# RWKV-7 scan of a two-layer diffusion backbone: r stored beside the keys, the values' chunk halves exchanged when they are written, the in-context rates of both directions in one tensor

## The chip, the cores and the metric

The kernel runs on one core of a Trainium2 chip. The metric is the device time of one launch, in microseconds (us); lower is better. The time before the change is 2466.11 us, the median of three runs (2457.85, 2466.11 and 2469.48). Engines are named as the profile names them: PE (TensorE matmuls) and PEld (its weight loads), DVE (VectorE), ACT (ScalarE), POOL (GpSimd) and SP (SyncE, which here issues nearly all transfers; its rows in the trace are marked SPq).

## What is computed

Layer 0 is attention, layer 1 is a bidirectional RWKV-7 time mixing beside a Hyena convolution. All arithmetic is float32. The change touches layer 1's RWKV branch alone: 8 heads of width 64, 1024 latent tokens behind 256 context tokens, both directions. Cut to what matters:

```python
def rwkv_features(u, w0, w_up, a0, a_up, k_k, k_a):
    r, k, v, dw_f, dw_b, da_f, da_b = split_cols(u, RWKV_SPLITS)
    kk = to_heads(k * k_k, RWKV_HEADS)
    kk = kk * lax.rsqrt(jnp.sum(kk * kk, axis=-1, keepdims=True) + 1e-12)
    for d, (dw, da) in enumerate(((dw_f, da_f), (dw_b, da_b))):
        w_log = -jax.nn.softplus(-(w0[d] + jnp.tanh(dw) @ w_up[d])) - 0.5
        decay = jnp.exp(-jnp.exp(w_log))
        a = jax.nn.sigmoid(a0[d] + da @ a_up[d])
        k_d = k * (1 + (a - 1) * k_a)
        dirs.append((decay, k_d, kk * a))
...
    def step(s, inp):                       # wkv_scan, per token, either direction
        sa = jnp.einsum('bhij,bhj->bhi', s, kk_t)
        s = s * w_t[:, :, None, :] - sa[..., None] * b_t[:, :, None, :] + v_t[..., None] * k_t[:, :, None, :]
        y = jnp.einsum('bhij,bhj->bhi', s, r_t) if emit else None
...
    yn = (yn * gn_w + gn_b)                 # rwkv_readout: group norm over a head, then the bonus
    bonus = jnp.sum(r * k_bonus * r_k, axis=-1, keepdims=True) * v
```

The context is scanned first; its final state starts the scan of the latent tokens. `k_bonus` is the mean of both directions' `k_d`, so the bonus needs r, k, v and both directions' a.

## The kernel before

The program is one instruction stream per engine, put in order ahead of the run by a scheduler that simulates a timeline and lists the ready instructions; a change in any transfer can therefore move instructions of all engines that follow it. Layer 1 ends with two stages that overlap.

**Projection (`gemm3`).** 128-column blocks of the input projection. `rw` makes one block of r, v or k after the token shift and writes it to DRAM. Blocks of v and r go to `US` (features by tokens, line 1125). Keys go through `rw_keys` to `KK`, a tensor [512 features, 5 blocks, 2, 256 tokens], where slot 0 holds the normalised keys kk and slot 1 the keys k (line 1318). `rw_values` transposes v to tokens by features and writes `VT` (line 1331). `rw_gates` writes the sigmoids of the decay (`SG`, one tensor per direction) and the in-context rates a (`AS`, one tensor per direction).

**Scan (`rwkv`).** There are 8 jobs, 4 head pairs j by 2 directions d, each of 5 blocks of 256 tokens (block 0 is the context): 40 blocks in all. Every block goes through

- `rw_front` (lines 1464 to 1576): loads kk and k (`kkf`, line 1475) and for the latent blocks r (line 1477), a (`af`), the decay (`sg`) and the values `V` (line 1486); makes chunk matrices of 64 tokens on PE, DVE, ACT and POOL; writes 32x32 blocks of the triangular system to DRAM (`LD`, line 1558). `V` is wanted with the two 64-token chunks of every 128 tokens exchanged between the halves of the partitions, and so is loaded by two transfers of 64 partitions;
- `rw_invert` (line 1578): reads the small blocks of a job back (`L<-LD`, line 1588) and inverts them by a loop of 31 steps on DVE, two instructions a step (`tmp`, line 1595, and `X`, line 1597); writes `XD` (line 1599). Job 0 is inverted in two parts, blocks 0 and 1 and then blocks 2 to 4;
- `rw_inverses` (line 1606): four loads of the inverse, `XT`; `rw_solve`: the solve (`y_ps`, `z_ps`, `R` on DVE at line 1629, `w_ps`), which also loads the values in both halves of `UV` (line 1617);
- `rw_trans`, `rw_own` and `rw_scan`: the transition matrices and the state's recurrence (`sy_ps` on PE, `S` on ACT), four chunks a block.

Up to 12 fronts run ahead of the scan. For the 16 latent blocks of direction 1, `rw_bonus` (line 1709) loads k, a of direction 0, a of direction 1, r, v and the gate g (line 1718), each as a tile of its own: `iok`, `ioa`, `iob` and `ior` share four buffers. POOL forms the bonus keys (lines 1721 to 1724), DVE multiplies r (line 1725), PE sums over a head (`bo_ps`). `rw_readout` normalises and, for j below 3, writes the high and the low half of the result by two transfers (line 1770). From block 28 on `Final` runs the output projection (`fe_ps`) between the scans.

SP issues its transfers in program order. A load whose buffer is still read holds everything behind it on SP.

Of the kernel before, what the change touches and what calls it, by code (L numbers as in the profile page):

```python
# [10 lines left out]
F32 = mybir.dt.float32  # L11
# [164 lines left out]
class K:  # L176
# [39 lines left out]
    def dt(self, shape, name, dt=F32):  # L216
        return self.dram.tile(shape, dt, name=name, tag=name)
# [781 lines left out]
    def layer1(self):  # L999
        nc, tc, a = self.nc, self.tc, self.a  # L1000
        dt = self.dt
        self.US = dt([13 * 128, NT], "US")
        self.G1 = dt([512, NL], "G1")
        self.HT = [dt([2, 8, 128, 512], "HT0"), dt([8, 128, 512], "HT1")]
        self.HF = dt([512, 4, 256], "HF")
        self.M1 = dt([2, 1024, NL], "M1")
        self.XC = dt([2, 128, KT, NC_], "XC")
        self.KK = dt([512, 5, 2, 256], "KK")
        self.VT = dt([NT, 512], "VT")
        self.AS = [dt([512, NT], f"AS{d}") for d in range(2)]  # L1010
        self.SG = [dt([NT, 512], f"SG{d}") for d in range(2)]
        with ExitStack():
            with ExitStack() as s2:
                xp = s2.enter_context(tc.tile_pool(name="l1x", bufs=1, reuse_waits="tile"))
                xl = [xp.tile([128, KT, NL], F32R, name=f"xl{p}") for p in range(2)]
                cst = ExitStack()
                xp = cst.enter_context(tc.tile_pool(name="l1c", bufs=1, reuse_waits="tile"))
                self.xc = [xp.tile([128, KT, NC_], F32R, name=f"xc{p}") for p in range(2)]

                def x(p, k, t0, n):  # L1020
                    return self.xc[p][:, k, t0:t0 + n] if t0 < NC_ else xl[p][:, k, t0 - NC_:t0 - NC_ + n]

                with ExitStack() as s3:
                    wp = s3.enter_context(tc.tile_pool(name="adap1", bufs=1, reuse_waits="tile"))
                    pp = s3.enter_context(tc.tile_pool(name="adaps1", bufs=2, space=PSUM, reuse_waits="tile"))
                    self.gemm2(x, wp, pp)
                self.wo_stack.close()
                for p in range(2):
                    nc.sync.dma_start(out=self.XC[p], in_=self.xc[p].bitcast(F32))
                cst.close()  # L1030
                self.gemm3(x)
            if self.stop == "gemm3":
                return
            self.rwkv()
# [21 lines left out]
    def gemm3(self, x):  # L1056
# [3 lines left out]
        with ExitStack() as st:  # L1060
# [44 lines left out]
            def rw(c0, b, ctx, w, sub):  # L1105
# [16 lines left out]
                if b // 4 == 1:  # L1122
                    self.rw_keys(b - 4, o, rp, pp)
                else:
                    nc.sync.dma_start(out=self.US[c0:c0 + 128, 0 if ctx else NC_:], in_=o)
                if b // 4 == 2:
                    self.rw_values(b - 8, o, rp, pp)

# [172 lines left out]
    def rw_keys(self, j, o, sp, pp):  # L1301
# [13 lines left out]
            nc.gpsimd.tensor_tensor(out=kk[:, s], in0=kk[:, s], in1=sq[:, 0:n], op=ALU.mult)  # L1315
        rows = slice(j * 128, j * 128 + 128)
        for i, t in enumerate((kk, o)):
            nc.sync.dma_start(out=self.KK[rows, :, i, :], in_=t.rearrange("p (q t) -> p q t", t=256))

    def rw_values(self, j, o, sp, pp):  # L1320

# [3 lines left out]
        for t4 in range(0, 10, 4):  # L1325
# [2 lines left out]
            for q in range(m):  # L1328
                nc.tensor.matmul(ps[:, q, :], o[:, (t4 + q) * 128:(t4 + q + 1) * 128], self.cent, start=True, stop=True)
            self.evac(vt[:, t4:t4 + m, :], ps[:, 0:m, :])  # L1330
        nc.sync.dma_start(out=self.VT[:, j * 128:j * 128 + 128].rearrange("(t p) f -> p t f", p=128), in_=vt)

    def rw_gates(self, sp, pp):

# [129 lines left out]
    def rw_front(self, F, q, wp, bufs):  # L1464
# [7 lines left out]
        K0 = math.exp(-0.5)  # L1472

        kk = fp.tile([128, 3, 256], F32, name="kkf", bufs=2)
        nc.sync.dma_start(out=kk[:, 1:3], in_=self.KK[rows, q])
        if lat:
            nc.sync.dma_start(out=kk[:, 0], in_=self.US[rows, q * 256:q * 256 + 256])
        af = fp.tile([128, 256], F32, name="af", bufs=3)
        nc.sync.dma_start(out=af, in_=self.AS[d][rows, q * 256:q * 256 + 256])
        sg = fp.tile([128, 2, 128], F32, name="sg", bufs=3)  # L1480
        tok = slice(q * 256, q * 256 + 256)
        nc.sync.dma_start(out=sg, in_=self.SG[d][tok, rows].rearrange("(t p) f -> p t f", p=128))
        V = fp.tile([128, 2, 128], F32, name="V", bufs=2)
        vsrc = self.VT[tok, rows].rearrange("(i c p) f -> c p i f", c=2, p=64)
        for c in range(2):
            nc.sync.dma_start(out=V[64 * c:64 * c + 64], in_=vsrc[1 - c])
        sgs = fp.tile([128, 2, 2, 128], F32R, name="sgs", bufs=2)
        self.split(sgs[:, 0], sgs[:, 1], sg)

# [118 lines left out]
    def rw_solve(self, F, q, n):  # L1608
# [5 lines left out]
        rows = slice(F["j"] * 128, F["j"] * 128 + 128)  # L1614
        vsrc = self.VT[q * 256:q * 256 + 256, rows].rearrange("(i c p) (h f) -> c p i h f", c=2, p=64, h=2)
        for c in range(2):
            nc.sync.dma_start(out=UV[64 * (1 - c):64 * (1 - c) + 64, :, c], in_=vsrc[c])

        def prod(w, x, name):
            ps = self.rps([128, 4, 128], name, "s", PB[0])  # L1620
# [88 lines left out]
    def rw_bonus(self, j, q):  # L1709
# [1 line left out]
        nc, C, wp = self.nc, self.C, self.wp  # L1711
        rows, tok = slice(j * 128, j * 128 + 128), slice(q * 256, q * 256 + 256)
        io = []
        for n, src in (("k", self.KK[rows, q, 1, :]), ("a", self.AS[0][rows, tok]), ("b", self.AS[1][rows, tok]),
                       ("r", self.US[rows, tok]), ("v", self.US[1024 + j * 128:1152 + j * 128, tok]),
                       ("g", self.G1[rows, q * 256 - 256:q * 256])):
            t = wp.tile([128, 256], F32, name=f"io{n}", tag="iovg" if n in "vg" else "io", bufs=4)
            nc.sync.dma_start(out=t, in_=src)
            io.append(t)
        k, a0, a1, r, v, g = io  # L1720
        nc.gpsimd.tensor_tensor(out=a0, in0=a0, in1=a1, op=ALU.add)
        nc.gpsimd.tensor_scalar(out=a0, in0=a0, scalar1=0.5, scalar2=-1.0, op0=ALU.mult, op1=ALU.add)
        nc.gpsimd.tensor_scalar(out=a0, in0=a0, scalar1=self.col("rwkv_k_a", j), scalar2=1.0, op0=ALU.mult, op1=ALU.add)
# [7 lines left out]
    def rw_readout(self, j, q, Y, vg):  # L1731
# [31 lines left out]
        if j == 3:  # L1763
            m = self.m3[q]
            self.split(m[:, 0], m[:, 1], t)
            return
        m = [wp.tile([128, 256], F32R, name="m1", tag="m1", bufs=3) for _ in range(2)]
        self.split(m[0], m[1], t)
        for p in range(2):
            nc.sync.dma_start(out=self.M1[p, j * 128:j * 128 + 128, q * 256 - 256:q * 256], in_=m[p].bitcast(F32))  # L1770


    def reduced_sin(self, out, ps, bias, pool):
# [398 lines left out]
```

## Time and profile before

| what | us |
|---|---|
| median of three runs | 2466.11 |
| the profiled execution's own time | 2463.09 |
| its span (first to last instruction) | 2461.3 |
| PE busy in the span | 2212.4 (90%) |
| PEld / DVE / ACT / POOL busy | 1839.0 / 1548.4 / 1103.4 / 927.3 |

The page's shares are averages over stages with different limits. The scan's fronts begin at about 1763 us, the first solve at about 1861 us, the output projection mixes in from about 2250 us. A view by stages (stretches of time with each engine's busy time, the granted PE clock as a part of full speed, and the DMA engines' mean busy share) tells them apart. The chain of waits follows the work that ended last back from the last instruction; a piece "SPq L1477" in it is the time in which SP issued that transfer, and "DMA kkf<-US" the time from the issue to its landing.

### The profile page before, as it was taken

The page shows a single profiled execution, that of the slowest core. Times are in us where ns is not written, and L with a number is a line of the kernel's source. Part 1 is how long each engine was busy: PE and PEld are TensorE (multiplying, and loading weights), DVE is VectorE, ACT ScalarE, POOL GpSimd, SP SyncE. Part 2 cuts the span into 40 slices and gives each one's busy share as a digit, 9 for nine tenths or more (in the row PEclk, how much of TensorE's full clock was granted, in tenths as well). Part 3 has the DMA queues.
Part 4 walks back from the last instruction along what each step waited for, and adds up shares of the span by engine and source line. Part 5 has one row for each costly group of instructions (what it writes and reads, how often), then busy time and mean ns, then how long its engine had stood idle before and what let it go on. Part 6 is the DMA issues. An engine that isn't in the chain of part 4 may idle for free. (4 is left out here: it accounts for less than half of the span.)

```text
span 2461.3 us, 45979 instructions
## 1 busy us (share of the span) xinstructions
PE 2212.4 (90%) x17167; PEld 1839.0 (75%) x17167; DVE 1548.4 (63%) x3091; ACT 1103.4 (45%) x2403; POOL 927.3 (38%) x959
## 2 busy tenths in 40 slices
PE   4999999999999998689899999899968888988897
PEld 3877788677877887577788787788756777777685
DVE  6255532368768877454476877566788886767524
ACT  5354434456556555532232232255444455555224
POOL 1253335301011545511132333323564555556512
PEclk8999999999999999899999999999968899998898
DMA  8433344673222666834443464474443444444522
GB/s 283 133 124 118 125 144 146 194 234 121 85 74 70 193 196 185 241 116 168 154 146 119 147 207 145 152 237 154 146 130 86 129 126 127 114 129 134 172 84 93
DMA packets 351573, 361.79 MB, mean 147 GB/s; under 512 B 83122, under 2 KB 283199, under 8 KB 350582
## 3 DMA queue, kind: packets, MB, share of 16 engines
q1 hardware_dynamic: 342038, 330.40, 44.3%
q10 hardware_dynamic: 9168, 24.25, 3.2%
q0 software_dynamic: 144, 4.19, 0.4%
q8 instruction: 136, 2.23, 0.4%
q14 instruction: 87, 0.71, 0.1%
HBM read 260.14 MB, written 100.10 MB: 146 GB/s over the span
## 5 line engine op out<-in xcount | busy, mean ns | idle before, releaser
L160 PE MATMUL g_ps<-xl,w_hi 128*128 128x512 f32 x1056 | 269.0, 401 | 1.0 <-ACT w_hi L194 1.0
L160 PEld LDWEIGHTS g_ps<-xl,w_hi 128*128 128x128 f32 x1056 | 200.1, 192 | 44.6 <-issue 2.4
L160 PE MATMUL s_ps<-k,q 128*128 128x256 f32 (+1 forms) x704 | 199.1, 379 | 7.3 <-DVE pn L702 4.0
L443 POOL TENSOR_TENSOR al_acc<-al_acc,al_t 128x512 f32<-128x512 f32 x98 | 128.8, 1314 | 186.5 <-ACT al_t L441 135.9
L198 DVE TENSOR_TENSOR w_lo<-w_raw,w_hi 128x256 fp32r<-128x256 f32 (+1 forms) x184 | 126.8, 745 | 85.3 <-PE g_ps L160 44.2
L189 ACT COPY pt<-pt_ps 128x512 f32<-128x512 f32 (+1 forms) x203 | 101.7, 505 | 137.6 <-PE pt_ps L163 131.7
L1595 DVE TENSOR_TENSOR tmp<-L,X 80x112 f32<-80x112 f32 (+28 forms) x279 | 136.9, 491 | 25.4 <-DMA L<-LD 17.0
L1597 DVE TENSOR_TENSOR X<-X,tmp 80x112 f32<-80x112 f32 (+28 forms) x279 | 136.1, 488 | 6.6
L160 PE MATMUL g_ps<-xl,w_lo 128*128 128x512 f32 x528 | 137.4, 394 | 0.0
L163 PE MATMUL pt_ps<-ident,p 128*128 128x128 f32 x704 | 119.2, 285 | 17.0 <-DVE pt L187 7.1
L160 PE MATMUL g_ps<-xhi,w_hi 128*128 128x512 f32 (+1 forms) x528 | 118.3, 366 | 8.9 <-DVE ac_res L285 4.7
L163 PEld LDWEIGHTS pt_ps<-ident,p 128*128 128x128 f32 x704 | 81.6, 143 | 52.5 <-DVE pt L187 14.2
L160 PEld LDWEIGHTS s_ps<-k,q 128*128 128x128 f32 x704 | 108.9, 198 | 14.5 <-DVE p L702 7.3
L697 ACT ACTIVATE p<-p,mn 128x1280 f32<-128x1280 f32 (+1 forms) x96 | 103.4, 1078 | 35.7 <-DVE p L702 35.6
L160 PE MATMUL g_ps<-xhi,w_lo 128*128 128x512 f32 (+1 forms) x528 | 119.0, 364 | 0.0
L883 POOL TENSOR_TENSOR bias<-namask,tt 128x384 f32<-128x384 f32 x64 | 67.7, 1059 | 129.9 <-DVE mn L892 54.1
L441 ACT ACTIVATE al_t<-al_w,condT 128x512 f32<-128x512 f32 x98 | 70.8, 722 | 98.9 <-POOL al_acc L443 62.3
L160 PEld LDWEIGHTS g_ps<-xl,w_lo 128*128 128x128 f32 x528 | 98.9, 189 | 20.9 <-issue 0.7
L160 PE MATMUL g_ps<-xlo,w_hi 128*128 128x512 f32 (+1 forms) x528 | 113.0, 356 | 0.0
L160 PEld LDWEIGHTS g_ps<-xhi,w_hi 128*128 128x128 f32 x528 | 89.9, 193 | 29.6 <-DVE qraw L551 5.4
L160 PEld LDWEIGHTS g_ps<-xhi,w_lo 128*128 128x128 f32 x528 | 89.8, 191 | 18.9 <-issue 5.8
L160 PEld LDWEIGHTS g_ps<-xlo,w_hi 128*128 128x128 f32 x528 | 89.6, 191 | 15.8 <-issue 1.9
(432 smaller groups left out, 5708.4 us busy)
## 6 DMA issues: line engine op xcount, KB each, us to landing
w_raw<-rec_w_in SPq DMA_DIRECT2D x33, 512.0 KB
hfw<-FW SPq DMA_DIRECT2D x32, 512.0 KB
w_raw<-attn_w_in SPq DMA_DIRECT2D x13, 1024.0 KB
al_w<-rec_ada_w SPq DMA_DIRECT2D x48, 256.0 KB
tt<-TG SPq DMA_DIRECT2D x64, 192.0 KB
kkf<-KK SPq DMA_DIRECT2D x40, 256.0 KB
q<-qb SPq DMA_DIRECT2D x64, 128.0 KB
HS<-hs SPq DMA_DIRECT2D x32, 256.0 KB
```

The lines of the kernel that those rows point to most:

```text
L160: return self.keep(self.pe.matmul(*args, **kw))
L163: return self.keep(self.pe.transpose(*args, **kw))
L189: self.nc.scalar.copy(out=out, in_=in_)
L198: e.tensor_tensor(out=lo, in0=full, in1=hi.bitcast(F32), op=ALU.subtract)
L441: nc.scalar.activation(out=o, in_=wt, func=AF.Copy, scale=self.condT[:, k, ci:ci + 1])
L443: nc.gpsimd.tensor_tensor(out=t, in0=t, in1=o, op=ALU.add)
L697: self.nc.scalar.activation(out=p, in_=p, func=AF.Exp, bias=mn, scale=-1.0, accum_out=rs)
L883: nc.gpsimd.tensor_tensor(out=b, in0=mask, in1=tt, op=ALU.subtract)
L1595: nc.vector.tensor_tensor(out=tv, in0=L[:, s:s + 1, rt].to_broadcast([n, nj, nt]), in1=X[:, rj, s:s + 1].to_broadcast([n, nj, nt]), op=ALU ...
L1597: nc.vector.tensor_tensor(out=X[:, rj, rt], in0=X[:, rj, rt], in1=tv, op=ALU.subtract)
```

## The change

1. `KK` becomes [512, 5, 3, 256]: slot 0 takes r (latent blocks only), slots 1 and 2 kk and k. The four r blocks are written there rather than to `US`. A latent front loads r, kk and k by one transfer of 384 KB, where it loaded 256 KB and 128 KB.
2. The chunk halves are exchanged when `VT` is written (two transfers of 64 partitions in place of one of 128, four times). A front loads `V` by one transfer of 128 partitions; `UV` still takes two, with the halves named the other way round.
3. `AS` becomes one tensor [2, 512, tokens]. The bonus loads r and k by one transfer and both rates by one: four transfers of 128 KB become two of 256 KB, into two buffers of twice the size.
4. The readout's high and low halves go out by one transfer (tile `m1`, two buffers of 256 KB for three of 128 KB).

```diff
-        self.KK = dt([512, 5, 2, 256], "KK")
+        self.KK = dt([512, 5, 3, 256], "KK")
-        self.AS = [dt([512, NT], f"AS{d}") for d in range(2)]
+        self.AS = dt([2, 512, NT], "AS")
...
-                    nc.sync.dma_start(out=self.US[c0:c0 + 128, 0 if ctx else NC_:], in_=o)
+                    if ctx:
+                        nc.sync.dma_start(out=self.US[c0:c0 + 128, :], in_=o)
+                    else:
+                        nc.sync.dma_start(out=self.KK[c0:c0 + 128, 1:5, 0, :], in_=o.rearrange("p (q t) -> p q t", t=256))
...
-            nc.sync.dma_start(out=self.KK[rows, :, i, :], in_=t.rearrange("p (q t) -> p q t", t=256))
+            nc.sync.dma_start(out=self.KK[rows, :, i + 1, :], in_=t.rearrange("p (q t) -> p q t", t=256))
...
-        nc.sync.dma_start(out=self.VT[:, j * 128:j * 128 + 128].rearrange("(t p) f -> p t f", p=128), in_=vt)
+        for c in range(2):
+            nc.sync.dma_start(out=self.VT[:, j * 128:j * 128 + 128].rearrange("(t c p) f -> c p t f", c=2, p=64)[1 - c],
+                              in_=vt[64 * c:64 * c + 64])
...
-        nc.sync.dma_start(out=kk[:, 1:3], in_=self.KK[rows, q])
-        if lat:
-            nc.sync.dma_start(out=kk[:, 0], in_=self.US[rows, q * 256:q * 256 + 256])
+        nc.sync.dma_start(out=kk if lat else kk[:, 1:3], in_=self.KK[rows, q] if lat else self.KK[rows, q, 1:3])
...
-        vsrc = self.VT[tok, rows].rearrange("(i c p) f -> c p i f", c=2, p=64)
-        for c in range(2):
-            nc.sync.dma_start(out=V[64 * c:64 * c + 64], in_=vsrc[1 - c])
+        nc.sync.dma_start(out=V, in_=self.VT[tok, rows].rearrange("(i p) f -> p i f", p=128))
...
-            nc.sync.dma_start(out=UV[64 * (1 - c):64 * (1 - c) + 64, :, c], in_=vsrc[c])
+            nc.sync.dma_start(out=UV[64 * (1 - c):64 * (1 - c) + 64, :, c], in_=vsrc[1 - c])
...
-        for n, src in (("k", self.KK[rows, q, 1, :]), ("a", self.AS[0][rows, tok]), ("b", self.AS[1][rows, tok]),
-                       ("r", self.US[rows, tok]), ("v", self.US[1024 + j * 128:1152 + j * 128, tok]),
-                       ("g", self.G1[rows, q * 256 - 256:q * 256])):
-            t = wp.tile([128, 256], F32, name=f"io{n}", tag="iovg" if n in "vg" else "io", bufs=4)
+        for n, src in (("rk", self.KK[rows, q, 0:3:2, :]), ("ab", self.AS[:, rows, tok].rearrange("d p t -> p d t"))):
+            t = wp.tile([128, 2, 256], F32, name=f"io{n}", tag="io", bufs=2)
+            nc.sync.dma_start(out=t, in_=src)
+            io += [t[:, 0], t[:, 1]]
+        for n, src in (("v", self.US[1024 + j * 128:1152 + j * 128, tok]), ("g", self.G1[rows, q * 256 - 256:q * 256])):
+            t = wp.tile([128, 256], F32, name=f"io{n}", tag="iovg", bufs=4)
             nc.sync.dma_start(out=t, in_=src)
...
-        m = [wp.tile([128, 256], F32R, name="m1", tag="m1", bufs=3) for _ in range(2)]
-        self.split(m[0], m[1], t)
-        for p in range(2):
-            nc.sync.dma_start(out=self.M1[p, j * 128:j * 128 + 128, q * 256 - 256:q * 256], in_=m[p].bitcast(F32))
+        m = wp.tile([128, 2, 256], F32R, name="m1", tag="m1", bufs=2)
+        self.split(m[:, 0], m[:, 1], t)
+        nc.sync.dma_start(out=self.M1[:, j * 128:j * 128 + 128, q * 256 - 256:q * 256].rearrange("p f t -> f p t"), in_=m.bitcast(F32))
```

What the change does to the order is shown at three places. Line numbers are each kernel's own: in the changed one `kkf` is loaded at line 1481, `af` at 1483, `sg` at 1486, `V` at 1488, `UV` at 1619, the bonus at 1718 and 1722, and the readout writes at 1773. A number behind a name (`AS_12036`) tells tensors of one name apart.

**SP, the loads of the first two fronts (a context block, then a latent one).** Before:

```order
L1475 DMA kkf<-KK 128x512
L1479 DMA af<-AS_12036 128x256
L1482 DMA sg<-SG_12038 128x2x128
L1486 DMA V<-VT 64x2x128 x2
L1475 DMA kkf<-KK 128x512
L1477 DMA kkf<-US 128x256
L1479 DMA af<-AS_12036 128x256
L1482 DMA sg<-SG_12038 128x2x128
L1486 DMA V<-VT 64x2x128 x2
```

Now:

```order
L1481 DMA kkf<-KK 128x512
L1483 DMA af<-AS 128x256
L1486 DMA sg<-SG_12037 128x2x128
L1488 DMA V<-VT 128x2x128
L1483 DMA af<-AS 128x256
L1481 DMA kkf<-KK 128x768
L1486 DMA sg<-SG_12037 128x2x128
L1488 DMA V<-VT 128x2x128
```

A latent front now has four loads on SP where it had six.

**SP, around the fourth bonus of job 1 (in the trace at about 1955 us), up to its load of the rates.** Before:

```order
L1475 DMA kkf<-KK 128x512
L1477 DMA kkf<-US 128x256
L1479 DMA af<-AS_12037 128x256
L1486 DMA V<-VT 64x2x128 x2
L1606 DMA XT_17594<-XD_17621 32x4x32 x4
L1475 DMA kkf<-KK 128x512
L1479 DMA af<-AS_12036 128x256
L1718 DMA ioa<-AS_12036 128x256
L1718 DMA iob<-AS_12037 128x256
L1479 DMA af<-AS_12036 128x256
L1617 DMA UV<-VT 64x2x128 x2
L1718 DMA ior<-US 128x256
```

Now (this bonus's `iork` was issued far ahead, among the fronts):

```order
L1481 DMA kkf<-KK 128x768
L1483 DMA af<-AS 128x256
L1486 DMA sg<-SG_12037 128x2x128
L1560 DMA LD_19018<-la 32x4x32 x4
L1722 DMA iov<-US 128x256
L1619 DMA UV<-VT 64x2x128
L1590 DMA L<-LD_19018 80x1024
L1722 DMA iog<-G_12028 128x256
L1619 DMA UV<-VT 64x2x128
L1773 DMA M_12032<-m_19684 128x2x256
L1718 DMA ioab<-AS 128x2x256
```

The load of r, which stood behind the rates, is gone from here.

**DVE, around the first solve's R.** Before:

```order
L1543 TENSOR_TENSOR la<-g_ps,gm 128x256 x2
L1597 TENSOR_TENSOR X<-X,tmp 48x20x12
L1595 TENSOR_TENSOR tmp<-L,X 48x231
L1597 TENSOR_TENSOR X<-X,tmp 48x21x11
L1629 TENSOR_TENSOR R<-R,z_ps 128x512
L1595 TENSOR_TENSOR tmp<-L,X 48x220
```

Now:

```order
L1597 TENSOR_TENSOR tmp<-L,X 48x87
L1599 TENSOR_TENSOR X<-X,tmp 48x29x3
L1597 TENSOR_TENSOR tmp<-L,X 48x60
L1631 TENSOR_TENSOR R<-R,z_ps 128x512
L1599 TENSOR_TENSOR X<-X,tmp 48x30x2
L1523 TENSOR_TENSOR BK<-af,E 128x2x2x64
```

The R of the first solve has moved from the middle of the second inversion's loop to its end. Counted from the first `tmp`, 104 instructions of the loop and 32 others stood before it, and now 121 and 40; for the sixth R it was 200 and 75, and now 199 and 72.

## Rows read from the trace of the kernel before

**Rows 1.** Stretches: length, busy us (xinstructions) per engine, PE clock, DMA share.

```profile
core 0: us, PE busy (x) PEld busy (x) DVE busy (x) ACT busy (x) POOL busy (x), PEclk, DMA share, GB/s
1700.00:1770.00 70.00, 70.00 (x311) 56.18 (x311) 53.10 (x50) 29.81 (x55) 33.51 (x33) 1.00 0.40 129
1770.00:1850.00 80.00, 54.39 (x390) 43.58 (x390) 65.75 (x126) 35.03 (x104) 57.03 (x72) 0.68 0.47 131
1850.00:2050.00 200.00, 171.33 (x2247) 142.48 (x2246) 160.10 (x361) 103.13 (x316) 109.46 (x159) 0.90 0.43 117
2050.00:2250.00 200.00, 176.89 (x2476) 147.72 (x2476) 140.72 (x327) 110.42 (x342) 117.94 (x173) 0.93 0.45 122
2250.00:2462.00 212.00, 183.88 (x1655) 143.59 (x1654) 104.51 (x208) 69.52 (x193) 76.12 (x96) 0.91 0.40 121
```

**Rows 2.** Issues of touched transfers in the chain: start us, us, what.

```profile
1911.80 0.42 SPq L1477
...
1912.27 0.43 SPq L1718
...
1955.27 0.43 SPq L1477
...
1957.22 0.60 SPq L1486
...
1961.35 0.43 SPq L1718
...
2024.05 0.58 SPq L1477
...
2056.29 0.61 SPq L1486
...
2069.87 0.61 SPq L1486
...
2114.49 0.45 SPq L1770
...
2137.72 0.43 SPq L1477
...
2181.38 0.43 SPq L1477
```

**Rows 3.** The chain's two waits for r.

```profile
1966.05 4.14 DMA ior<-US
...
2075.67 4.01 DMA ior<-US
```

**Rows 4.** DVE's timeline at the reader of r: start, us, instruction, idle before.

```profile
1970.31 0.48 DVE L1725 SCALAR_TENSOR_TENSOR ioa<-ioa,vec,ior 128x256 f32<-128x256 f32 x1 [2.92 <-DMA ior<-US]
...
2079.78 0.48 DVE L1725 SCALAR_TENSOR_TENSOR ioa<-ioa,vec,ior 128x256 f32<-128x256 f32 x1 [0.65 <-POOL gm L1547]
```

**Rows 5.** V behind XT: SP's timeline at its first half.

```profile
1946.09 0.58 SPq L1486 DMA_DIRECT2D V<-VT  x1
```

**Rows 6.** The chain at V's second half.

```profile
1948.77 1.95 DMA V<-VT
```

**Rows 7.** SP's issues by tile or line: ns min/median/max, first and last start.

```profile
L1477 SPq DMA_DIRECT2D kkf<-US x32: 422/430/1818, 1766.3 to 2217.6; - x32
L1486 SPq DMA_DIRECT2D V<-VT x80: 573/598/1346, 1764.3 to 2224.1; - x80
L1482 SPq DMA_DIRECT2D sg<-SG x40: 370/420/1159, 1763.8 to 2189.6; - x40
L1718 SPq DMA_DIRECT2D iob<-AS x16: 319/430/584, 1834.8 to 2348.5; - x16
```

**Rows 8.** Who waited for whom, 1770 to 2462 us: us, times, longest.

```profile
POOL ioa L1721 <- DMA iob<-AS: 35.9, 9, 9.1
```

**Rows 9.** DVE groups, 1770 to 2462 us: busy us, mean ns, idle before.

```profile
L1595 DVE TENSOR_TENSOR tmp<-L,X 80x112 f32<-80x112 f32 (+28 forms) x279 | 136.9, 491 | 25.4 <-DMA L<-LD 17.0 <-POOL X L1590 1.9
L1543 DVE TENSOR_TENSOR la<-g_ps,gm 128x256 f32<-128x256 f32 x80 | 31.2, 413 | 7.2 <-PE g_ps L160 6.9
```

More of the change, by code (lines that the diff above doesn't have):

```diff
@@ L1713, in rw_bonus @@
         io = []
-        for n, src in (("k", self.KK[rows, q, 1, :]), ("a", self.AS[0][rows, tok]), ("b", self.AS[1][rows, tok]),
-                       ("r", self.US[rows, tok]), ("v", self.US[1024 + j * 128:1152 + j * 128, tok]),
-                       ("g", self.G1[rows, q * 256 - 256:q * 256])):
-            t = wp.tile([128, 256], F32, name=f"io{n}", tag="iovg" if n in "vg" else "io", bufs=4)
+        for n, src in (("rk", self.KK[rows, q, 0:3:2, :]), ("ab", self.AS[:, rows, tok].rearrange("d p t -> p d t"))):
[4 more added lines that the diff above has]
+            t = wp.tile([128, 256], F32, name=f"io{n}", tag="iovg", bufs=4)
             nc.sync.dma_start(out=t, in_=src)
             io.append(t)
-        k, a0, a1, r, v, g = io
+        r, k, a0, a1, v, g = io
         nc.gpsimd.tensor_tensor(out=a0, in0=a0, in1=a1, op=ALU.add)
```

## Prediction

> **What bounds the kernel now.** I read the stretches first [rows 1]. All that the change touches lies behind about 1630 us. From 1700 to 1770 us, still projection, PE is busy for 70.00 of 70 us: what is added to SP or written there is covered by PE's own work. From 1770 to 1850 us PE is busy for 54.39 of 80 and DVE for 65.75: DVE bounds, with the loop of the first inversion. From 1850 to 2250 us no engine is full: PE has 171.33 and 176.89 of 200 each, DVE 160.10 and 140.72. Blocks go from engine to engine here, and the end is set by whatever each hand-over waits for. After 2250 us PE leads again, with the output projection and 183.88 of 212.
>
> The 400 us in the middle have 52 us of idle PE, so this is where fewer transfers can pay. The DMA engines are not the limit, at a share of 0.43 and 0.45. What can be late is SP, which issues in order, one transfer about every half microsecond. The chain of waits shows it: eleven times it runs through the issue of a transfer that the change removes [rows 2], on the way to a load behind it on SP. Twice it waits for the bonus's r [rows 3], once for the second half of V [rows 6].
>
> **The change part by part.**
>
> *Issues that go.* 32 loads of r into fronts at 0.430, 40 second halves of V at 0.598, 32 of the bonus's loads at 0.430, and 12 writes of the readout, for which the chain's 0.45 serves [rows 2, 7]: 13.8 + 23.9 + 13.8 + 5.4 = 56.9 us of SP's time. The V that stays has the shape of sg (128 partitions, two pieces of 512 bytes each), at 0.420 for 0.598 [rows 7], another 40 x 0.178 = 7.1. Most of the 64 us lies beside other work, since SP mostly works ahead. On the path are the eleven issues: three seconds of V, 0.60 + 0.61 + 0.61 = 1.82; five loads of r, 0.42 + 0.43 + 0.58 + 0.43 + 0.43 = 2.29; two first rates, 0.43 each, 0.86; one write, 0.45 [rows 2]. That is 5.42, or **5.4 us**. They stand one behind the other in front of the load that ended the wait, so I take them whole; at the least, where something else was as late, they are worth nothing.
>
> *V behind XT.* At 1946.09 us the first half of V is issued, then four XT loads that wait for PE, and only at 1948.77 the second half, on which the chain waits [rows 5, 6]. One transfer goes at 1946.09: up to 2.68 earlier. The chain reaches this place by way of PE, so something else is not far behind; I take **2.0**.
>
> *The bonus's r.* Before, r shares four buffers with k and the two rates, is issued behind them, and waits for a buffer that POOL's first addition frees. The chain waits for it 4.14 and 4.01 us [rows 3]. Now it comes with k, ahead of the rates, and that wait has no place any more. What is late next: DVE itself stood idle for 2.92 us for the first of these loads, but for the second it was then released by POOL's gm, 0.65 us after its last instruction [rows 4]. DVE's idle time is what comes back, 2.92 + 0.65 = 3.57, **3.6**; the ceiling is 8.15.
>
> *The rates as one transfer.* POOL waits for the second rate 35.9 us in nine waits, 9.1 the longest [rows 8]. One issue less per pair is counted above; the wait itself stays, since POOL reaches its addition before a load issued at that place can land. POOL is in order, and the fronts' BK and gm are queued behind the addition, which PE's g_ps and bk_ps wait for. I price this at nothing; at the best half of the wait goes, 18 us.
>
> *Added work.* Four more writes of VT, at V's 0.598 [rows 7] 2.4 us, lie where PE never idles [rows 1]; uncovered they would cost those 2.4. The r blocks are written in pieces of 1 KB for 4 KB, four times, in the same cover. A larger `kkf` lands at once where kk and k came ahead of r; it is double buffered and read a front later, and POOL is not seen waiting for kkf. No engine's instruction count changes beside SP's.
>
> *Moved work.* The scheduler has put fronts and bonuses ahead. In front of the first R of a solve DVE now has 17 more instructions of the inversion's loop and 8 others, but none more by the sixth R (the order on DVE). At 0.491 for one of the loop and 0.413 for a mask [rows 9] the first R comes 8.3 + 3.3 = 11.6 us later, and that is caught up within five blocks, because the same work is then missing behind it. I count nothing for the end.
>
> **Sum:** 5.4 + 2.0 + 3.6 = 11.0 us; with every wait at its ceiling 5.4 + 2.7 + 8.2 = 16.3. Against the profiled execution's own 2463.09 us this gives 2452.1. That execution lies 3.0 us under the median of the runs, so for the median it is 2466.1 - 11.0 = **2455 us**.
>
> A sentence apart on a page that speaks against the change. The DMA engines have a share of 0.43 to 0.47 in the scan [rows 1], so they are more than half idle. The Trainium skill, Perfetto Trace Analysis, section DMA Optimizations, says that splitting transfers "may allow some to start sooner" where the DMA engines are generally idle, which would make joining them the wrong direction here. By the rows, SP's issue and the order on it stand in the chain and the engines' share does not, so I keep the sum; the result by the page's rule is the last rival below.
>
> **The rivals.**
>
> *Nothing reaches the end.* The chain is one path among several nearly as late: PE, DVE and the inversion's chain through DRAM (DVE waits 17.0 us for L<-LD in the same stretch [rows 9], which the change does not touch). For it: PE's and DVE's shares both over 0.7 to 0.85, so that a wait removed is often followed by another engine's. Against it: the two waits for r end on DVE alone. Time: 2466 us.
>
> *More comes back.* With 64 us less on SP, half of POOL's 35.9 us goes as well, and the terms reach their ceilings: 16.3 + 18 = 34, 2432 us. For it: nine waits of four us each are late issues as much as landings. Against it: POOL has time to spare, 117.94 of 200 busy.
>
> *The start is pushed back, slower.* The first R comes 11.6 us later on DVE, where DVE bounds (65.75 of 80 [rows 1]), and a bonus now stands there on POOL, whose wait for the pair is like the rates' mean, 35.9 / 9 = 4.0. If the 40 blocks of the scan follow each other without slack from the first one on, both stay to the end: 2466 + 15.6 = 2482 us. It decides if DVE and PE have no idle time between the first and the sixth solve in which to catch up; they have some 20% and 14% [rows 1].
>
> *Joined loads land late, slower.* Both of a pair are held until the later part is free and landed. Landings in the chain range from 1.95 us for V to 4.14 for r [rows 3, 6]; if each of the nine waits of POOL grew by this difference, 2.2 us, and nothing else hid it, the cost is 9 x 2.2 = 19.8 and the time 2486 us. It decides if POOL is found waiting for kkf, which it is not now. By the page's rule above this is the outcome, and the trace before shows the idle engines but no such wait.
>
> **How the numbers follow.** About 0.5%, 12.3 us, is what a measurement of this kernel can tell from no change: 2453.8 to 2478.4. The forecast, 2455 (2447 to 2463, since the order of many instructions changes with it), has 0.44; more comes back 0.15; nothing 0.20; the start pushed back 0.13; joined loads late 0.08. Faster by over 0.5%: two fifths of the forecast's own (0.18), all of "more", a quarter of "nothing" (0.05, for the reordering) and 0.02 of the rest: 0.40. Slower by over 0.5%: 0.11 and 0.07 of the two slow cases and 0.02 of "nothing", 0.20. The same: 0.40. The range leaves out the ends of the outer cases: 2432 to 2484 us.
>
> **What would show it.** Right: in the chain of the changed kernel no piece of L1481 of r's own, V once per front with issues near 0.42; DVE's wait at the bonus's product (now line 1729) for a DMA near zero instead of several us a time; PE's busy time per 200 us between 1850 and 2250 up by some 5, the stage shorter by about 11. Wrong: POOL waiting for `ioab` for more than 36 us or for `kkf` at all; the first solve more than 10 us later and the later ones not back at their times; or the same stage length with the idle time of PE now before DVE's la or ACT's S.

## The result

The changed kernel takes 2455.61 us, the median of 14 runs (2444.39 to 2467.47); the kernel before takes 2466.82 beside it, also in 14 runs (2457.85 to 2478.49). The ratio is 0.9950, with a 95% interval of 0.9933 to 0.9966: 11.2 us faster, between 8.4 and 16.5. The forecast was 2455. The number holds. Several of its reasons do not, or are not shown; the runs below sort some of them, and which part of the change makes the gain stays open.

A caution on the traces first. The profiled execution of the changed kernel has a time of its own of 2460.39 us, 4.8 above its median; that of the kernel before, 2463.09, lies 3.7 below its median. The two profiles differ by 2.7 us where the medians differ by 11.2. A second profile of the changed kernel (2449.23 us) is therefore read beside the first.

**The scan as a whole.** Stretches from the first load of a front to the end, columns as in [rows 1]: the kernel before, the changed kernel, and its second profile.

```profile
core 0: us, PE busy (x) PEld busy (x) DVE busy (x) ACT busy (x) POOL busy (x), PEclk, DMA share, GB/s
1762.00:2461.00 699.00, 594.50 (x6798) 484.01 (x6796) 475.13 (x1029) 320.24 (x957) 366.97 (x505) 0.89 0.44 123
```

```profile
1764.00:2458.00 694.00, 601.28 (x6797) 487.30 (x6796) 479.33 (x1028) 320.93 (x957) 371.20 (x505) 0.89 0.45 124
```

```profile
1758.00:2447.00 689.00, 594.62 (x6797) 480.97 (x6796) 476.96 (x1028) 320.24 (x957) 373.10 (x505) 0.90 0.45 125
```

The work is the same (6797 matmuls for 6798). What fell is PE's idle time: 699 - 594.5 = 104.5 us before, 92.7 and 94.4 after, 10 to 12 us less. The first profile gives part of it back, since its matmuls take 6.8 us longer in all.

The idle time of one profile does not give a kernel's time, though. The same stretch in four kernels of the experiments below: the kernel before with V exchanged alone, the kernel before with r listed first, the kernel before with parts 1 and 3, and the changed kernel with V in halves again.

```profile
1768.00:2468.00 700.00, 605.57 (x6795) 490.56 (x6793) 480.36 (x1027) 319.76 (x957) 372.81 (x505) 0.88 0.44 123
```

```profile
1760.00:2462.00 702.00, 610.50 (x6796) 496.26 (x6794) 473.08 (x1028) 321.08 (x957) 366.36 (x505) 0.87 0.44 122
```

```profile
1769.00:2461.00 692.00, 589.08 (x6795) 478.15 (x6793) 475.93 (x1028) 320.35 (x957) 372.16 (x505) 0.90 0.45 124
```

```profile
1762.00:2447.00 685.00, 585.57 (x6793) 474.26 (x6792) 478.00 (x1027) 320.30 (x957) 372.77 (x505) 0.91 0.45 125
```

The first two have as little idle time as the change, 94.4 and 91.5 us, but longer matmuls at a lower granted clock, and by their ratios they can't be told from the kernel before. The last two have 102.9 and 99.4 us, but shorter matmuls, and are faster than it.

**Where PE's idle time fell.** The changed kernel in the stretches of [rows 1]:

```profile
1770.00:1850.00 80.00, 64.72 (x443) 50.80 (x441) 64.81 (x115) 39.76 (x117) 64.86 (x80) 0.68 0.56 158
1850.00:2050.00 200.00, 165.64 (x2143) 138.18 (x2142) 162.06 (x368) 99.02 (x303) 103.89 (x146) 0.86 0.40 105
2050.00:2250.00 200.00, 178.44 (x2425) 147.77 (x2423) 142.12 (x327) 106.16 (x327) 114.29 (x166) 0.92 0.44 118
2250.00:2459.00 209.00, 186.49 (x1767) 145.59 (x1764) 107.23 (x215) 74.11 (x209) 83.73 (x110) 0.95 0.44 130
```

Against [rows 1] PE gains 10.3 us of work in the first 80 us (64.72 for 54.39) and has 22.5 us of idle time for 28.1 at the end. In the 400 us in the middle its idle time is 55.9 us, for 51.8 before. The first of these differences goes with the order of the instructions and not with the time. In the changed kernel with V in halves again (below), whose scan begins within 1 us of that of the kernel before, PE is busy for 3.1 us less in the first 80 us than in the kernel before, and that kernel is no slower than the change by its ratio:

```profile
1770.00:1850.00 80.00, 51.30 (x353) 40.67 (x352) 67.31 (x133) 34.53 (x103) 56.56 (x71) 0.64 0.50 142
```

**The transfers.** SP's issues of kkf and of V, shape as in [rows 7]:

```profile
L1481 SPq DMA_DIRECT2D kkf<-KK x40: 320/365/1152, 1765.0 to 2227.0; - x40
L1488 SPq DMA_DIRECT2D V<-VT x40: 376/382/1504, 1766.5 to 2231.5; - x40
```

One V per front at 0.382 us, one kkf at 0.365. The lengths of SP's issues between 1850 and 2250 us add up to 292 us before and to 230 and 234 after. In the chain of that stretch five pieces of issues are left on the lines of V, the bonus and the readout (0.46 us at L1718, 0.34 at L1488, 0.30 and 0.38 at L1722, 0.38 at L1773; waits of 0.02 not counted), 1.9 us, and 2.6 us in the second profile. Before, these lines and the load of r had 7.2 us, of which [rows 2] lists the 5.4 that go.

**DVE at the bonus's product**, the group that read r [rows 4], in the kernel before and then in the changed one (busy us, mean ns, idle us before it and its releasers):

```profile
L1725 DVE SCALAR_TENSOR_TENSOR ioa<-ioa,vec,ior 128x256 f32<-128x256 f32 x16 | 9.2, 576 | 20.8 <-DMA ior<-US 17.3 <-POOL ioa L1724 2.9 <-POOL gm L1547 0.6
```

```profile
L1729 DVE SCALAR_TENSOR_TENSOR ioab<-ioab,vec,iork 128x256 f32<-128x256 f32 x16 | 11.2, 700 | 23.7 <-POOL ioab L1728 23.7
```

The wait for r is gone, and DVE waits no less: 23.7 us for 20.8 (20.9 in the second profile). The wait has changed hands, to POOL's last addition, and POOL stands behind the load of the rates, as before [rows 8]:

```profile
POOL ioab L1725 <- DMA ioab<-AS: 31.0, 7, 10.1
```

These are sums over 16 bonuses, on the path or not. In the chain of the changed kernel there is no wait for r, and of waits for the rates none in the first profile and one of 4.41 us in the second.

### The profile page after: what moved, and what is told of

It is laid out like the page before. It is cut to its first block, busy times and chain, and to the rows that moved or that the text cites. A ratio compares the mean times of both kernels' runs of the same rounds, so it can differ in the third digit from the quotient of the medians.

```text
span 2458.6 us, 45876 instructions
## 1 busy us (share of the span) xinstructions
PE 2214.9 (90%) x17167; PEld 1837.9 (75%) x17167; DVE 1549.7 (63%) x3091; ACT 1103.1 (45%) x2403; POOL 931.1 (38%) x959
## 5 line engine op out<-in xcount | busy, mean ns | idle before, releaser
L1597 DVE TENSOR_TENSOR tmp<-L,X 80x112 f32<-80x112 f32 (+25 forms) x279 | 137.4, 492 | 18.8 <-DMA L<-LD 10.5
L1599 DVE TENSOR_TENSOR X<-X,tmp 80x112 f32<-80x112 f32 (+25 forms) x279 | 137.1, 491 | 7.0
L160 PEld LDWEIGHTS g_ps<-xl,w_lo 128*128 128x128 f32 x528 | 98.6, 188 | 20.8 <-issue 0.7
```

Of the source, the lines that this page charges most:

```text
L160: return self.keep(self.pe.matmul(*args, **kw))
L1597: nc.vector.tensor_tensor(out=tv, in0=L[:, s:s + 1, rt].to_broadcast([n, nj, nt]), in1=X[:, rj, s:s + 1].to_broadcast([n, nj, nt]), op=ALU ...
L1599: nc.vector.tensor_tensor(out=X[:, rj, rt], in0=X[:, rj, rt], in1=tv, op=ALU.subtract)
```

## Experiments

Every kernel was timed beside the kernel before, on the same chip. The groups of runs lie on two chips or more, so ratios to the kernel before are compared, not medians.

**The four parts, each alone on the kernel before.** Part 1, r beside the keys (the bonus still with four loads of its own):

```diff
-        nc.sync.dma_start(out=kk[:, 1:3], in_=self.KK[rows, q])
-        if lat:
-            nc.sync.dma_start(out=kk[:, 0], in_=self.US[rows, q * 256:q * 256 + 256])
+        nc.sync.dma_start(out=kk if lat else kk[:, 1:3], in_=self.KK[rows, q] if lat else self.KK[rows, q, 1:3])
```

> Part 1 alone on the kernel before: r lies beside the keys and a latent front loads both at once; V, the bonus's four loads and the readout's two writes stay. Theory (SP's issues and the waits behind them are what the change gives back): the five pieces of r in the chain go, 2.3 us, so about 2464 against 2466.8, ratio 0.999. Rival A (the new list order, not the transfers, makes the difference): anywhere from 2450 to 2480, with no relation to the issues saved. Rival B (joined loads land late): slower, and POOL or DVE waiting for kkf where they did not before.

Measured: 2470.84 us, 1.0011 (0.9996 to 1.0026). The theory's 0.999 lies outside.

Part 2, the chunks exchanged where VT is written, one load of V:

```diff
-        for c in range(2):
-            nc.sync.dma_start(out=V[64 * c:64 * c + 64], in_=vsrc[1 - c])
+        nc.sync.dma_start(out=V, in_=self.VT[tok, rows].rearrange("(i p) f -> p i f", p=128))
```

> Part 2 alone on the kernel before: the chunk halves are exchanged when VT is written, V is loaded by one transfer. Theory (SP's issues): the three second halves in the chain, 1.8 us, and the place behind XT, 2.0 us, so about 2463, ratio 0.9985; the one V is issued in about 0.42 us. Rival A (list order): anywhere from 2450 to 2480.

Measured: 2466.40 us, 0.9993 (0.9978 to 1.0009).

Part 3, both rates by one load; r and k by two loads into a tile of their own:

```diff
+        t = wp.tile([128, 2, 256], F32, name="ioab", tag="io", bufs=2)
+        nc.sync.dma_start(out=t, in_=self.AS[:, rows, tok].rearrange("d p t -> p d t"))
```

> Part 3 without part 1 on the kernel before: both rates in one tensor and one load, r and k still two loads but into one tile of their own, so that r no longer takes a buffer that POOL has to free. Theory (the wait of the bonus's r is a real cost): DVE's wait for r (17.3 us in five waits before) nearly gone, 3.6 us and two issues of 0.43 come back, so about 2462, ratio 0.998. Rival A (list order): anywhere from 2450 to 2480.

Measured: 2462.18 us, 0.9983 (0.9966 to 1.0000).

Part 4, the readout's two halves by one write:

```diff
-        for p in range(2):
-            nc.sync.dma_start(out=self.M1[p, j * 128:j * 128 + 128, q * 256 - 256:q * 256], in_=m[p].bitcast(F32))
+        nc.sync.dma_start(out=self.M1[:, j * 128:j * 128 + 128, q * 256 - 256:q * 256].rearrange("p f t -> f p t"), in_=m.bitcast(F32))
```

> Part 4 alone on the kernel before: the readout's two halves written by one transfer, 12 issues fewer. Theory (SP's issues): one issue of 0.45 us in the chain, so no change, 2466, ratio 1.000. Rival A (list order): as this edit takes away almost nothing, a difference of 5 us or more either way would be the order's doing alone.

Measured: 2467.00 us, 0.9993 (0.9975 to 1.0011).

The four add up to 2.0 thousandths, 4.9 us, for the 11.2 of the whole. Only part 3 shows anything by itself, and its interval just reaches 1.0000. So, by the ratios, either the parts need each other or the gain is an accident of the order.

**Parts 1 and 3 together**, which lets r and k of the bonus come by one load as well:

```diff
+        for n, src in (("rk", self.KK[rows, q, 0:3:2, :]), ("ab", self.AS[:, rows, tok].rearrange("d p t -> p d t"))):
+            t = wp.tile([128, 2, 256], F32, name=f"io{n}", tag="io", bufs=2)
+            nc.sync.dma_start(out=t, in_=src)
```

> Parts 1 and 3 of the change together on the kernel before (r beside the keys, rates in one tensor, so that the bonus's r and k come by one load too); the values and the output write as before. Parts 1 and 3 apart gave 1.0011 and 0.9983, with r and k still two loads. Theory (SP's issues): 32 kkf issues and 32 of the bonus's gone, some 27 of 64 us, 4.7 us faster: 2462, 0.998. Rival C (the gain is in the joined load of r and k that only both parts allow): nearly all of the change's gain, 2456, 0.9955. Rival A (order): no relation.

Measured: 2453.65 us for 2463.06, 0.9961 (0.9941 to 0.9981), 9.6 us faster. That is near rival C and inside the theory's reach. By the ratios, then, most of the change's 11.2 us is in the loads of r, k and the rates. What is left for V and the readout's write is 1.6 us by these figures and 5.9 by the second measurement of the changed kernel below (0.9937); neither can be told from nothing. POOL's wait for the rates is the shortest of all here, 17.1 us for 35.9 in [rows 8]:

```profile
POOL ioab L1725 <- DMA ioab<-AS: 17.1, 8, 7.6
```

But the profiled execution took 2463.17 us, 9.5 above this kernel's median, and PE's idle time in it is close to that of the kernel before (102.9 us, above). So this profile does not show where the 9.6 us come from.

**The changed kernel again**, as the base for what is built on it:

> The changed kernel again, as the base for the two kernels below that are built on it. Theory (SP's issue time on the path): 2456 us, 0.995 of the kernel before, as measured already. Nothing else is asked of it; the scatter of its profile against its median is.

Measured: 2452.91 us, 0.9937 (0.9915 to 0.9959). SP's issues of kkf in its profile:

```profile
L1481 SPq DMA_DIRECT2D kkf<-KK x40: 326/376/1616, 1759.0 to 2214.8; - x40
```

The first of them stands at 1759.0, and at 1765.0 in the first profile of the same code, above. Six microseconds between two executions arise ahead of the scan; no single pair of profiles settles 5 us here.

**kkf in two loads again**, keys first, on the changed kernel:

```diff
-        nc.sync.dma_start(out=kk if lat else kk[:, 1:3], in_=self.KK[rows, q] if lat else self.KK[rows, q, 1:3])
+        nc.sync.dma_start(out=kk[:, 1:3], in_=self.KK[rows, q, 1:3])
+        if lat:
+            nc.sync.dma_start(out=kk[:, 0], in_=self.KK[rows, q, 0])
```

> The changed kernel with kkf filled by two loads from KK, keys first and r second, in the 32 fronts that read r: 32 more issues of about 0.4 us, 13 us of SP's time. Theory: 13 of 64 us of issues, 2.2 us slower than the changed kernel, 2458. Rival B (a joined load comes late, since its first 2 KB wait for the third; part 1 alone gave 1.0011 of the kernel before, no gain, and the chain of the changed kernel holds 11.9 us of kkf<-KK in four pieces): the keys come sooner, up to 8 us faster than the changed kernel, 2448. Rival A: any of these, by the order.

Measured: 2457.38 us, 0.9965 (0.9947 to 0.9983), 4.5 us above the changed kernel on the same chip. Rival B wanted it faster by up to 8. So no loss by joined loads that land late is seen here; split, they cost something, at the edge of what can be told. The rule of the Trainium skill, Perfetto Trace Analysis, section DMA Optimizations (where the DMA engines are generally idle, splitting transfers may let the whole complete sooner), is not borne out by this run, with the engines' share at 0.45 in the stretch above.

**V in two halves again**, on the changed kernel, the exchange in DRAM kept:

```diff
-        nc.sync.dma_start(out=V, in_=self.VT[tok, rows].rearrange("(i p) f -> p i f", p=128))
+        vhalf = self.VT[tok, rows].rearrange("(i c p) f -> c p i f", c=2, p=64)
+        for c in range(2):
+            nc.sync.dma_start(out=V[64 * c:64 * c + 64], in_=vhalf[c])
```

> The changed kernel with V loaded in two halves of 64 partitions again, 40 more issues; the exchange of the chunks in DRAM stays. One issue of about 0.38 us becomes two of 0.3 us each by the kernel before, so 40 x 0.22 to 40 x 0.8 us, 9 to 32 us of SP's time. Theory: 1.5 to 5.5 us above the changed kernel, 2457 to 2461. Rival A: no relation; part 2 alone on the kernel before gave 0.9993.

Measured: 2450.07 us, 0.9935 (0.9911 to 0.9960): no slower by the ratio, though SP's issues rise from some 232 to 273 us of the 400 in the middle. Its runs had a higher clock, 0.9475 in the mean for 0.9446; the section on the clock below comes back to this. The trace adds one thing. DVE's timeline at the first solve's R (start us, us, [idle before]), in the kernel before, the changed kernel, and this one:

```profile
1867.85 0.69 DVE L1629 TENSOR_TENSOR R<-R,z_ps 128x512 f32<-128x512 f32 x1 [0.65 <-PE z_ps L160]
...
1945.07 0.68 DVE L1629 TENSOR_TENSOR R<-R,z_ps 128x512 f32<-128x512 f32 x1
```

```profile
1884.21 0.69 DVE L1631 TENSOR_TENSOR R<-R,z_ps 128x512 f32<-128x512 f32 x1
...
1942.86 0.69 DVE L1631 TENSOR_TENSOR R<-R,z_ps 128x512 f32<-128x512 f32 x1 [1.88 <-PE z_ps L160]
```

```profile
1867.73 0.69 DVE L1633 TENSOR_TENSOR R<-R,z_ps 128x512 f32<-128x512 f32 x1
...
1939.30 0.69 DVE L1633 TENSOR_TENSOR R<-R,z_ps 128x512 f32<-128x512 f32 x1 [0.67 <-PE z_ps L160]
```

With V in halves the scheduler puts the first solve back where it was, 16.5 us ahead of the changed kernel's (2.9 of it an earlier start of the scan). The sixth, the second row of each, comes within 4 us of the changed kernel's, and the time is the same by the ratio. So no gain or loss is seen from where the first solves stand, unless the added issues hide it.

**More issues on SP.** Into each front of the changed kernel four, then eight, transfers that nobody reads:

```diff
+        for _ in range(4):
+            ex = fp.tile([128, 2], F32, name="ex", bufs=8)
+            nc.sync.dma_start(out=ex, in_=self.KK[rows, q, 1, 0:2])
```

> The changed kernel with four more transfers in each front, each 128 partitions of two numbers, issued by SP between the loads and read by nobody: 160 issues, at the 0.38 us median of the kkf and V issues some 61 us of SP's time, nearly the 64 us that the change took away. Theory (SP's issue time is on the path, at 11 us for 64): 10.5 us slower than the changed kernel, 2466. Rival A (the gain is the new order that the scheduler made, not the issues): unrelated to the count, anywhere from 2448 to 2470, and a second look at the chain would show no more SPq than the changed kernel's 17.9 us from 1764 us on.

Measured with four: 2459.16 us, 0.9965 (0.9949 to 0.9980), 6.3 us above the changed kernel on the same chip, and still faster than the kernel before. SP's issues take 304 of the 400 us in the middle, more than the 292 before the change.

> The changed kernel with eight more tiny transfers in each front, 320 issues of 0.43 us, 138 us of SP's time, twice the dose of the kernel with four (which came 6.3 us above the changed kernel on the same chip). Theory (issues are on the path in part): at least twice that, 12.6 us above the changed kernel by the slope of the four, 24 by the prediction's 11 us for 64: 2466 to 2478, ratio 0.999 to 1.004. Rival A (order): no relation to the dose, 2450 to 2460.

Measured with eight: 2520.1 us, 1.0211 (1.0186 to 1.0236). The first 160 issues cost 2.8 thousandths (0.9965 against 0.9937), 6.9 us by the ratios, 0.04 each; the next 160 cost 24.6 thousandths, 60.7 us or 0.38 each, nearly the whole 0.43 us that one takes to issue. That is an engine that has run nearly full: SP issues for 329 of the 400 us, and its own waits in that stretch (added up over the view of SP's waits) fall to 48 us, from 170 in the changed kernel, 105 before and 81 with four. Who waits for whom, with eight:

```profile
POOL kd L1519 <- DMA af<-AS: 110.3, 30, 9.5
...
ACT sgs L194 <- DMA sg<-SG: 43.6, 25, 4.4
...
PE y_ps L160 <- DMA XT<-XD: 19.9, 11, 4.1
```

Now a front's own first loads are late, in 30 places on POOL and 25 on ACT. Page part 4, the chain's shares of the span, of the changed kernel and of this one:

```profile
PE 20%; DVE 12%; DMA 5%; issue 3%; ACT 1%; POOL 1%; SPq 1%; DVEq 0%; POOLq 0%; ACTq 0%
```

```profile
PE 20%; DVE 8%; DMA 6%; issue 3%; SPq 3%; POOL 3%; ACT 1%; POOLq 0%; DVEq 0%; ACTq 0%
```

SPq goes from 1% to 3%, POOL from 1% to 3%, and DVE's share shrinks. Added up from 1758 us on, SP's issues in the chain go from 17.9 to 83.0 us; transfers go from 68.8 to 94.8, so the landings may have a share too, which this run does not separate.

**The order alone.** The kernel before with the bonus's loads listed r first; the same transfers, but the order of every engine shifts:

```diff
-        for n, src in (("k", self.KK[rows, q, 1, :]), ("a", self.AS[0][rows, tok]), ("b", self.AS[1][rows, tok]),
-                       ("r", self.US[rows, tok]), ("v", self.US[1024 + j * 128:1152 + j * 128, tok]),
+        for n, src in (("r", self.US[rows, tok]), ("k", self.KK[rows, q, 1, :]), ("a", self.AS[0][rows, tok]),
+                       ("b", self.AS[1][rows, tok]), ("v", self.US[1024 + j * 128:1152 + j * 128, tok]),
```

> The kernel before with the bonus's loads written in another order: r first, then k, a, b, v, g. Same transfers and same bytes; the scheduler answers with another order on every engine, over 2600 lines of difference on PE. Theory: the order alone is worth nothing beyond what r's earlier arrival gives DVE (3.6 us by rows 3 and 4): 2463. Rival A (orders scatter by several us): off by more than 5 us from 2467 to either side.

Measured: 2467.35 us, 0.9992 (0.9975 to 1.0009): 2.0 us faster, between 6.2 faster and 2.2 slower. The 5 us of rival A are not seen, but the interval does not quite exclude them. The edit takes away DVE's wait for r as the change does, and the same thing takes its place:

```profile
DVE ioa L1725 <- POOL ioa L1724: 21.0, 6, 9.6
```

**XT's loads on ACT's queue**, on the changed kernel:

```diff
-            self.nc.sync.dma_start(out=self.C["XT"][n % NX][z, :, z], in_=xd[b])
+            self.nc.scalar.dma_start(out=self.C["XT"][n % NX][z, :, z], in_=xd[b])
```

> The changed kernel with the 160 loads of XT issued by ACT in place of SP: 69 us of SP's issue time go to ACT, which is busy for 321 of the 695 us of the stage and stands in its chain with 28 us. Theory (SP's issues are what costs): 6 to 12 us faster than the changed kernel, 2444 to 2450. Rival D (the issue costs wherever it stands, and ACT has evictions behind it that PE waits for): 2456 to 2465.

Measured: 2447.76 us, 0.9924 (0.9901 to 0.9948), the fastest ratio of all, but its interval overlaps the changed kernel's. It is 1.3 and 2.6 thousandths under the changed kernel's two ratios, 3 to 6 us, at or below the lower end of the theory's 6 to 12, with SP at 167 us of issues in the middle. From the scan's first load to the end it takes 2449.0 - 1770.3 = 678.7 us in its profile, for 693.6 and 688.5 in the changed kernel's two. That points to a second gain and doesn't prove it. Rival D is out: ACT takes the issues without loss.

**At the same clock.** Part of the scatter between runs goes with the mean clock granted to TensorE, which each run lists. Over the 82 runs of the kernel before in the three groups the time falls by 1.1 us per 0.001 of clock (correlation -0.62): the 13 runs below 0.939 have a mean of 2471.6 us, the 14 from 0.945 on 2461.1. The groups differ as well: at 0.942 the kernel before takes 2467.3, 2467.0 and, on the other chip, 2463.6 us. So each mean is moved along the line to 0.942 and set against the kernel before of its own group. The error is twice the standard error of both means; the line's own is not counted. The first measurement of the change has no clocks on record for the kernel before, so the second stands here.

| kernel | us to the kernel before, same clock, same group | error |
|---|---|---|
| part 1 | +1.7 | 2.6 |
| part 2 | -3.3 | 2.4 |
| part 3 | -6.3 | 2.9 |
| part 4 | -1.0 | 2.7 |
| parts 1 and 3 | -5.9 | 3.5 |
| the change, second measurement | -11.0 | 1.8 |
| kkf split | -7.5 | 1.9 |
| V split | -7.6 | 3.4 |
| four extra issues | -9.4 | 2.3 |
| r first | -5.1 | 3.0 |
| XT on ACT | -15.4 | 4.7 |

A kernel's clock may itself follow from its idle times, so this is a second reading and no verdict (eight extra issues, at a clock of 0.929, are left out for that reason). It agrees with the ratios on the change as a whole, and makes four extra issues nearly free (1.6 us for 160). On the parts it does not agree. Apart they add up to 8.9 of the 11.0 us; parts 1 and 3 give 5.9 us together and 4.6 apart, which is no difference; part 2 and r first come out clear of nothing; V in halves costs 3.4 us; and XT on ACT is 4.4 us below the change, within the errors.

## Why the prediction was right, and where its steps were not

**The issues, 5.4 us: the wrong measure.** The chain lost them, as said. But an issue in the chain is not worth its own length, and 64 us of SP's time are not worth a fixed fraction. The two tests of the dose show a flat stretch and a wall: 160 issues put in cost 7 us or less, and a kernel with more SP time than the one before is still faster than it; 160 more cost 0.38 each. The kernel before, at 292 of 400 us, lay within the first dose. Nor does a piece in the chain count in full: from 1758 us on, SP's issues in the chain are 39.4 us in the kernel before and 21.2 with part 2 alone, and the issues, transfers and POOL's pieces together 170.5 us before and 114.0 with r listed first, at times that can't be told from the kernel before by the ratios. The step failed as a mechanism, in "I take them whole". Its size is not refuted: the first dose put back about as much SP time as the change took away, for 6.9 us by the ratios and 1.6 at the same clock.

**V behind XT, 2.0 us (and V's 1.82 of the issues): over-sized by one reading, right by the other.** V alone gave 1.7 us with an interval from 5.4 faster to 2.2 slower, and split again it cost nothing by the ratio; at the same clock these are 3.3 and 3.4 us, near the 3.8 priced. The prediction also says that the chain waits once for V's second half; it does so twice:

```profile
1907.53 2.78 DMA V<-VT
```

**The bonus's r, 3.6 us: the wait was not removed but handed on, and what that is worth is not shown.** I read from one row with 2.92 and one with 0.65 us of idle time that DVE's wait comes back. Over all 16 bonuses it was 20.8 us before and 23.7 after, because POOL's additions behind the rates were nearly as late as r. The trace of before hides this: a wait goes to what came last, and r came last. The rows that I had, POOL's 35.9 us for the rates [rows 8], said it, since the product needs POOL's sum too. r listed first gave 2.0 us by the ratio (6.2 faster to 2.2 slower) and 5.1 at the same clock (error 3.0). Neither excludes 3.6, though its DVE waits for POOL 21.0 us.

**The rates, 0: the chain's own waits were left out.** As a sum POOL's wait changed little (31.0 us for 35.9, in seven for nine). But three of these waits stood in the chain before, 9.1 us, which the prediction does not list among the chain's waits:

```profile
1912.74 3.77 DMA iob<-AS
...
1961.82 3.26 DMA iob<-AS
...
2002.71 2.10 DMA iob<-AS
```

In the changed kernel the chain has none and 4.4 us of such waits in the two profiles. Part 3 is the one part that shows something alone by both readings (0.9983, and 6.3 us at the same clock). But it also gives r a tile that POOL need not free, so what the rates by themselves are worth, and with it whether 0 was too low, stays open.

**Added work, 0: nothing speaks against it.** The joined kkf is waited for 2.7 us by DVE and 1.7 by POOL, once each, which I had named as a sign against me; the kernel with kkf split has neither wait and is no faster.

**Moved work, 0: right.** The first R came 16.4 us later (11.6 were worked out; 2.2 of the rest is a later start of the scan), the sixth 2.2 us earlier than before. The test with V in halves, where the first R is back at its time, agrees by the ratio.

**The check by PE's busy time: wrong place.** I expected 5 us more per 200 us between 1850 and 2250, and PE has 344.08 there for 348.22; what it gained lies in the first 80 us, where the order sets it (above), and after 2250.

**The rivals.** "Nothing" is out by the interval, "more" by the time, "the start pushed back" by the sixth R. "Joined loads late" is out as a whole, though part 1 alone, at 1.0011, leans its way.

**What stays open.** By the ratios parts 1 and 3 gave 9.6 us together, and apart a loss of 2.7 and a gain of 4.2. The gap of 3.3 thousandths is hardly more than its uncertainty (three intervals of 1.5 to 2.0 thousandths, about 3 together), and at the same clock it is 1.3 us. If there is a gap, it may be the joined load of r and k, which only both allow, or the order that the scheduler makes of each; a kernel with both parts but r and k in two loads would tell, and it wasn't tried. So the total was right, and which terms made it is not shown. By the ratios the split was partly luck: V, the write and r were priced at 7.9 us and gave little, the loads of the bonus and of kkf at 3.2 and gave most. At the same clock V and r lie near their prices, and part 1, priced at 2.3 us for its issues, shows no gain by either reading.

## What to carry to other kernels

Before pricing a wait that a change removes, ask what else the waiting instruction needs, and look up how long the other input's producer waits: the profile names the last one only, and here 17.3 us of one wait became 23.7 us of the next. An issuing queue can cost little until it is nearly full and then nearly its whole issue time (here 0.04 us an issue up to 304 of 400 us, 0.38 beyond); read how much the queue itself still waits (here 105 of 400 us before, 48 at the wall) rather than count the issues that go. Where a scheduler re-orders everything after each edit, test the parts together as well as apart. And where the parts are worth a few us each, compare within one group of runs and at one clock before saying which of them gained.

## What the runs showed of the hardware

- A transfer of 128 partitions with two numbers each takes SP no less time to issue than one of 128 KB: 0.432 us at the median for the extra ones, 0.382 for V. What costs more is the form: V in halves of 64 partitions takes 0.598 us an issue, in the changed kernel with V split as in the kernel before [rows 7].

```profile
L1491 SPq DMA_DIRECT2D ex<-KK x160: 414/432/1935, 1771.6 to 2209.6; - x160
...
L1490 SPq DMA_DIRECT2D V<-VT x80: 573/598/1582, 1763.6 to 2219.6; - x80
```

- The same 6797 matmuls took 601.28 us of PE's time in one execution of the changed kernel and 594.62 in another, at a granted clock of 0.89 and 0.90 in the scan. So two executions of one code can differ by 6.7 us in the length of the same matmuls, as much as any part was worth.
